# Seven block products in place of eight for eleven blocks of a feed-forward, with an encoder layer's residual put by in DRAM

## The chip, the cores and the metric

The kernel runs on one core of one Trainium2 chip. The metric is the device time of one execution in microseconds (us). TensorE (PE) multiplies into PSUM, VectorE (DVE) and ScalarE (ACT) do element-wise work, GpSimd (POOL) does some of it and issues the DMAs that add into SBUF, SyncE (SP) issues the plain DMAs.

## What is computed

One layer of a streaming encoder for 544 tokens (512 of a prompt and 32 of a sample) of width 1024. Three residual steps follow one another: a feed-forward, a mixer with two head groups, and a second feed-forward. The part that matters here is the last:

```python
def modulate(x, shift, scale):
    return x * (1.0 + scale[:, None, :]) + shift[:, None, :]

def post_norm(x, out, gate, weight, g, b):
    return layer_norm(ALPHA * x + weight * gate[:, None, :] * out, g, b)

def swiglu(h, w_gate, w_up, w_down):
    a = jnp.einsum('btd,df->btf', h, w_gate)
    u = jnp.einsum('btd,df->btf', h, w_up)
    return jnp.einsum('btf,fd->btd', jax.nn.silu(a) * u, w_down)
...
    x = post_norm(x, swiglu(modulate(x, sh3, sc3), f2_gate, f2_up, f2_down), 1.0 + gt3, 0.5, ln3_g, ln3_b)
```

The shifts, scales and gates come from a vector per request group times `w_cond`. `w_gate` and `w_up` are 1024 x 2816.

## The kernel before

Everything is float32. An operand of a product is split into two float32r parts, hi and lo, and a product is the sum of three matmuls, hi x hi, hi x lo and lo x hi (`mm3`, L139). The activations are kept turned, features on the partitions: `h` is eight tiles of 128 features by 2 parts by 544 tokens. A matmul has a 128x128 weight block as its stationary operand and 272 tokens (one half, `HALVES`) as the moving one, and PSUM gathers over the eight feature blocks.

The hidden width of 2816 is 22 blocks `f` of 128. For each block `ffn_up` (L193) makes four products of 24 matmuls, gate and up for both halves (`ffn_mm`, L172), and then `ffn_act` (L183) for each half: tanh of the gate on ACT (L187), two passes on DVE that make silu times up (L188, L189), a copy of its hi part on ACT (L190) and the lo part by subtraction on DVE (L191), into `hid[f]`. Blocks 0 and 1 of the second feed-forward are made together, half by half, by `k_outer` (L164), as `h` comes out of the layer norm. After block 21 the down products read all of `hid` (`proj_residual`, L205) and add into the residual `xr`.

Weights come through one queue, `stream`. `ensure` (L149) takes the next ones, loads them with SP into the pool `wr` (3 buffers), splits them with `split_w` (L123) into the pool `wh` (5 buffers), and `next_w` keeps three splits ahead. A split is a copy to hi on ACT (L129), minus hi into lo on ACT (L133), and a DMA issued by POOL that adds the raw weights from DRAM to lo (L134); with `lo_eng` a subtraction on that engine (L136) takes the place of the last two. Tiles of one size (4352 bytes per partition) share a pool `up` of 35 buffers: `h`, `hid`, `xr` and others. PSUM has eight banks, by tag: three a, two l, two t, one o.

The order of PE's instructions is that of the program (`ordered`, L66), and so is that of the loads on SP (`load`). On the other engines a planner orders the instructions by their place in the program and by when their inputs are due; `keep_in_program_order` pins an instruction behind the one written before it on its engine. Work beside the products is written as generators: `spawn` starts one, `tick` (L93), called after each product of 24 matmuls, moves on those that are due, and a `yield n` waits for n ticks.

Two such jobs run beside blocks 2 to 7 of the second feed-forward: `residual` (L1164), which scales the residual for the last layer norm with two POOL passes (L358) and two ACT passes (L360) per tile and four tiles, and `cond((8, (2, 3)))`, which loads eight tiles of `w_cond` and multiplies and adds them on DVE (L546) for the last gate.

Of the kernel before, what the change touches and what calls it, by code (L numbers as in the profile page):

```python
# [21 lines left out]
T = TP + TS  # L22
HT = T // 2
# [10 lines left out]
AHEAD = 3  # L34


@with_exitstack
def encoder_layer_kernel(ctx, tc, xT, cT, wc1, w_cond, b_condT, lnp, w_gu1, w_dn1, w_in, w_out, w_gu2, w_dn2,
                         ckT, cv, cikT, s0, cmat, ropes, dec, csm,
                         yT, akT, avT, ikT, st_p, st_s):  # L40
    nc = tc.nc
    ctx.enter_context(nc.allow_low_precision("operands are split exactly into two float32r parts"))
    const = ctx.enter_context(tc.tile_pool(name="const", bufs=1))
    up = ctx.enter_context(tc.tile_pool(name="up", bufs=35))
    wr = ctx.enter_context(tc.tile_pool(name="wr", bufs=3))
    wh = ctx.enter_context(tc.tile_pool(name="wh", bufs=5))
# [19 lines left out]
    def ordered(kind, r):  # L66
        if kind in last:
            tc.add_manual_dep(r.ins, last[kind], NOSYNC, reason="order of issue")
        last[kind] = r.ins.name

    def load(*a):
        ordered("load", nc.sync.dma_start(*a))

    def mm(*a, **kw):
        ordered("pe", nc.tensor.matmul(*a, **kw))  # L75
# [9 lines left out]
    def resume(job, base):  # L85
        n = next(job, None)
        if n is not None:
            jobs.append((base + n, job))

    def spawn(job):  # L90
        resume(job, now[0] + 1)

    def tick():  # L93
        now[0] += 1
        due = [j for t, j in jobs if t <= now[0]]
        jobs[:] = [x for x in jobs if x[0] > now[0]]
        for job in due:
            resume(job, now[0])
# [19 lines left out]
    def fetch_w(src, n, name):  # L118
        raw = wr.tile([P, ND, P], F32, name=f"wr_{name}", tag="wr")
        load(raw[:, :n, :], src)  # L120
        return raw

    def split_w(raw, n, name, lo_eng=None, pool=None, pin=False, src=None):  # L123
        if pool is None:
            hl = wh.tile([P, 2, ND, P], FR, name=f"wh_{name}", tag="wh")
            hi, lo = hl[:, 0], hl[:, 1]
        else:
            hi, lo = (pool.tile([P, ND, P], FR, name=f"wu_{name}", tag="u") for _ in range(2))
        c = nc.scalar.copy(hi[:, :n, :], raw[:, :n, :])  # L129
        if pin:  # L130
            tc.keep_in_program_order(c)
        if src is not None and lo_eng is None:
            nc.scalar.mul(lo[:, :n, :], hi[:, :n, :].bitcast(F32), -1.0)  # L133
            nc.gpsimd.dma_start(lo[:, :n, :], src, accum_op=ALU.add)  # L134
        else:
            (lo_eng or nc.gpsimd).tensor_tensor(lo[:, :n, :], raw[:, :n, :], hi[:, :n, :].bitcast(F32), op=ALU.subtract)  # L136
        return hi, lo
# [34 lines left out]
    def ffn_mm(st, h, which, i, tag=None):  # L172
        hls, banks = st
        if hls[which] is None:
            hls[which] = next_w()
        a, b = HALVES[i]
        ps = bank(tag or ("a" if which == 0 else "lt"[i]), f"gu{which}_{i}")[:, :HT]
        for k in range(ND):
            mm3(ps, hls[which], k, h[k], a, b, k == 0, k == ND - 1)
        banks[which, i] = ps  # L180
        tick()

    def ffn_act(st, hid, i):  # L183
# [3 lines left out]
        nc.scalar.activation(t, pg, AF.Tanh, scale=0.5)  # L187
        nc.vector.scalar_tensor_tensor(t, t, 1.0, pg, op0=ALU.add, op1=ALU.mult)  # L188
        nc.vector.tensor_tensor(t, t, pu, op=ALU.mult)  # L189
        nc.scalar.copy(hid[:, 0, a:b], t)  # L190
# [14 lines left out]
    def proj_residual(act, xr, coef, order, finish, need=(), ahead={}, final=None):  # L205
# [148 lines left out]
    def residual_next(xr, rs, al, j):  # L354

        for i, (a, b) in enumerate(HALVES):
            rb = rs[i].unsqueeze(1).to_broadcast([P, 2, HT])
            tc.keep_in_program_order(nc.gpsimd.tensor_tensor(xr[j][:, :, a:b], xr[j][:, :, a:b], rb, op=ALU.mult))  # L358
# [114 lines left out]
    for d in range(ND):  # L473
# [7 lines left out]
        if d in (0, 1, 3, 7):  # L481
            n = (0, 1, 3, 7).index(d)
# [51 lines left out]
    def cond(*parts):  # L534
        n = 0
        for m, pace in parts:
            acc = [up.tile([P, 1024], F32, name=f"ca{m}_{r}", tag="u") for r in range(2)]
            for d in range(ND):
                w = up.tile([P, 1024], F32, name=f"wc{m}_{d}", tag="u")
                load(w, w_cond[d * P:(d + 1) * P, 1024 * m:1024 * m + 1024])  # L540
                for r in range(2):
                    c = cz[:, d, r:r + 1]
                    if d == 0:
                        nc.vector.tensor_scalar(acc[r], w, c, None, op0=ALU.mult)
                    else:
                        nc.vector.scalar_tensor_tensor(acc[r], w, c, acc[r], op0=ALU.mult, op1=ALU.add)  # L546
# [7 lines left out]
    hid = []  # L554
# [27 lines left out]
    xd = nc.dram_tensor("x_spill", [4, P, 2 * T], F32, kind="Internal").ap()  # L582
# [567 lines left out]
    h, rs, fin = ln_to_h(xr, G3, B3, "h3_", 3, 4)  # L1150
# [172 lines left out]
```

## Time and profile before

| | |
|---|---|
| median of 3 runs | 1194.61 us (1192.08 to 1195.61) |
| the profiled execution's own time | 1194.37 us |
| its span, first to last instruction | 1192.2 us |
| mean granted TensorE clock | 0.989 |
| PE busy | 1162.6 us, 98% of the span, 9427 matmuls |
| DVE, ACT, POOL busy | 666.8, 586.8 and 206.5 us |
| products of blocks 0 and 1, second feed-forward | up to 802.66 us |
| blocks 2 to 21 | 802.66 to about 1043.5 us |
| its down products | from there to about 1177 us |

A row of a group of instructions gives the line, engine, operation, the tiles written and read, the shapes and the count, then busy time in us and the mean duration of one in ns, then how long the engine was idle just before them and what ended most of that. A row of the timeline gives start and duration in us, and in brackets the idle time before and its releaser.

### The profile page before, as it was taken

The numbers are of one execution on the slowest core, as the hardware profiler recorded it, in microseconds if no ns is written. First come the engines' busy times: TensorE is split into PE (matmuls) and PEld (weight loads), VectorE is DVE, ScalarE is ACT, GpSimd is POOL, SyncE is SP. The second block draws the span as 40 slices with busy tenths as digits, with TensorE's granted clock in tenths as the row PEclk, the third lists the DMA queues.
The fourth block names the chain that finished last, engine by engine and source line by source line (L and its number), as shares of the span: only waits on it lengthen the run. The fifth ranks groups of instructions, "written<-read, shape, count | busy, mean of one in ns | idle before, by whom it ended". The sixth has DMA issues, their size and how long they took to land.

```text
span 1192.2 us, 22987 instructions
## 1 busy us (share of the span) xinstructions
PE 1162.6 (98%) x9427; PEld 1129.9 (95%) x9427; DVE 666.8 (56%) x1567; ACT 586.8 (49%) x987; POOL 206.5 (17%) x234
## 2 busy tenths in 40 slices
PE   8999999999999999899989999999999999999995
PEld 6999999999999999789979989999999999999995
DVE  5756574763468394677887775896542222201416
ACT  3544444444334454655565678546444444433423
POOL 1311111111111303322110101105111111111110
PEclk9999999999999999899989999999999999999998
DMA  9899999987999557544845588817987888788842
GB/s 364 295 303 275 243 266 233 244 220 176 299 258 227 129 203 186 135 116 116 200 96 156 126 267 216 201 48 191 265 179 173 177 174 174 164 172 177 176 86 76
DMA packets 70953, 231.93 MB, mean 195 GB/s; under 512 B 8544, under 2 KB 12768, under 8 KB 70848
## 3 DMA queue, kind: packets, MB, share of 16 engines
q0 software_dynamic: 23616, 83.90, 40.4%
q1 hardware_dynamic: 47088, 146.43, 35.2%
q8 instruction: 74, 1.21, 0.4%
q14 instruction: 31, 0.25, 0.1%
q10 hardware_dynamic: 144, 0.14, 0.0%
HBM read 221.06 MB, written 7.35 MB: 192 GB/s over the span
## 4 chain that ended last, share of the span: by engine, by line
PE 90%; DVE 4%; DMA 3%; ACT 1%; issue 1%; SPq 0%; DVEq 0%; ACTq 0%
PE gu L75 41%; PE dn L75 26%; PE in L75 14%; PE gu_e L75 2%; DMA wc<-in_wc 1%; PE po L75 1%; PE pt L78 1%; DMA xr<-in_xT 1%; PE ro L75 1%; DMA rp<-iqf 1%; PE lg L75 1%; PE isc L75 1%; ACT wh_w L129 0%; DMA cm<-in_cmat 0%; DVE wk L790 0%
## 5 line engine op out<-in xcount | busy, mean ns | idle before, releaser
L75 PE MATMUL gu<-h,wh_w 128*128 128x272 f32 x3840 | 482.5, 288 | 0.0
L75 PEld LDWEIGHTS gu<-h,wh_w 128*128 128x128 f32 x3840 | 481.4, 188 | 0.0
L75 PE MATMUL dn<-hid,wh_w 128*128 128x272 f32 x2112 | 266.7, 288 | 0.0
L75 PEld LDWEIGHTS dn<-hid,wh_w 128*128 128x128 f32 x2112 | 265.4, 188 | 0.2
L129 ACT CAST wh_w<-wr_w 128x1024 fp32r<-128x1024 f32 (+1 forms) x162 | 165.8, 1024 | 148.0 <-PE dn L75 101.7
L75 PE MATMUL in<-h,wh_w 128*128 128x272 f32 x1392 | 190.7, 295 | 0.0
L75 PEld LDWEIGHTS in<-h,wh_w 128*128 128x128 f32 x1392 | 180.4, 192 | 5.3 <-issue 3.4
L133 ACT ACTIVATE wh_w<-wh_w 128x1024 fp32r<-128x1024 f32 x159 | 164.7, 1037 | 2.9
L546 DVE SCALAR_TENSOR_TENSOR ca<-wc,cz,ca 128x1024 f32<-128x1024 f32 x98 | 128.7, 1339 | 24.7 <-DMA wc<-in_w_cond 24.6
L134 POOL DMA_DIRECT2D wh_w<-in_w_gu x80 | 70.1, 876 | 415.8 <-ACT wh_w L133 356.6
L189 DVE TENSOR_TENSOR tnh<-tnh,gu 128x272 f32<-128x272 f32 x81 | 35.4, 437 | 129.5 <-PE gu L75 129.5
L187 ACT ACTIVATE tnh<-gu 128x272 f32<-128x272 f32 x80 | 31.9, 399 | 115.2 <-PE gu L75 115.2
L190 ACT CAST hid<-tnh 128x272 fp32r<-128x272 f32 x88 | 36.8, 419 | 93.9 <-DVE tnh L189 93.8
L188 DVE SCALAR_TENSOR_TENSOR tnh<-tnh,gu 128x272 f32<-128x272 f32 x80 | 34.7, 436 | 85.8 <-ACT tnh L187 85.6
L134 POOL DMA_DIRECT2D wh_w<-in_w_dn x48 | 41.7, 869 | 224.0 <-ACT wh_w L133 219.9
L269 DVE SCALAR_TENSOR_TENSOR xq<-dn,C,xq 128x272 f32<-128x272 f32 (+2 forms) x48 | 18.0, 403 | 105.0 <-PE dn L75 105.0
L191 DVE TENSOR_TENSOR hid<-tnh,hid 128x272 fp32r<-128x272 f32 x88 | 38.6, 440 | 37.2 <-ACT hid L190 36.8
L134 POOL DMA_DIRECT2D wh_w<-in_w_in x29 | 25.5, 893 | 135.2 <-ACT Pu L950 29.5
L789 DVE MAX8 m<-wk 128x8 f32<-128x544 f32 (+3 forms) x65 | 38.8, 597 | 0.7
L790 DVE MATCH_REPLACE8 wk<-m,wk 128x544 f32<-128x544 f32 (+3 forms) x65 | 38.0, 584 | 0.0
L75 PE MATMUL dn<-mx,wh_w 128*128 128x272 f32 x192 | 25.1, 289 | 0.0
L75 PE MATMUL in<-h,wu_w 128*128 128x272 f32 x192 | 24.6, 289 | 0.0
(274 smaller groups left out, 1118.4 us busy)
## 6 DMA issues: line engine op xcount, KB each, us to landing
wr_w<-in_w_gu SPq DMA_DIRECT2D x84, 512.0 KB, 5.2
wh_w<-in_w_gu POOLq DMA_DIRECT2D x80, 512.0 KB, 7.2
wc<-in_w_cond SPq DMA_DIRECT2D x56, 512.0 KB, 6.5
wr_w<-in_w_in SPq DMA_DIRECT2D x33, 512.0 KB, 5.2
wh_w<-in_w_in POOLq DMA_DIRECT2D x29, 512.0 KB, 6.8
wr_w<-in_w_dn SPq DMA_DIRECT2D x32, 448.0 KB, 4.1
wh_w<-in_w_dn POOLq DMA_DIRECT2D x32, 448.0 KB, 5.8
wc<-in_wc SPq DMA_DIRECT2D x16, 512.0 KB, 10.4
```

The costliest lines, as they stand in the source:

```text
L75: ordered("pe", nc.tensor.matmul(*a, **kw))
L129: c = nc.scalar.copy(hi[:, :n, :], raw[:, :n, :])
L133: nc.scalar.mul(lo[:, :n, :], hi[:, :n, :].bitcast(F32), -1.0)
L134: nc.gpsimd.dma_start(lo[:, :n, :], src, accum_op=ALU.add)
L187: nc.scalar.activation(t, pg, AF.Tanh, scale=0.5)
L188: nc.vector.scalar_tensor_tensor(t, t, 1.0, pg, op0=ALU.add, op1=ALU.mult)
L189: nc.vector.tensor_tensor(t, t, pu, op=ALU.mult)
L190: nc.scalar.copy(hid[:, 0, a:b], t)
L191: nc.vector.tensor_tensor(hid[:, 1, a:b], t, hid[:, 0, a:b].bitcast(F32), op=ALU.subtract)
L546: nc.vector.scalar_tensor_tensor(acc[r], w, c, acc[r], op0=ALU.mult, op1=ALU.add)
L789: behind(nc.vector.max(m8, w), "pe")
L790: nc.vector.match_replace(w, in_to_replace=m8, in_values=w, imm_value=MARK)
```

## The change

For blocks 4 to 14 (`SEVEN`) the gate and the up product of a block for both halves are taken together as a 2x2 by 2x2 block product: the weights are gate and up by lower and upper four feature blocks, the activations are lower and upper four feature blocks by first and second half. Eight block products of 12 matmuls become seven, by Winograd's scheme with sums of weights and sums of activations. `activation_sums` makes eight tiles of sums from `h` once. For each block `weight_sums` makes four sums on DVE in place, in the raw tiles, after `make_up` has copied and negated the upper half of up; `split_sums` splits the sums by a copy on ACT and a subtraction on DVE; `make_gate` splits the whole gate as before. Products share PSUM banks: the first product of a block stays in bank A, ACT takes a snapshot of it, and the next product adds into the same bank, three times over; B takes two products, C one. Every instruction of ACT and DVE in these blocks is pinned in the order written.

Besides, `xr` is written to DRAM six ticks after block 1 (`put_by`), and `bring_back` loads it again after block 19 and does the residual's scaling then; `cond` for the last gate starts after block 15 instead of block 2; and the low parts of the gates of blocks 15 to 21 and the up of block 15 are subtracted by DVE. The diff, cut where a reader can do without:

```diff
     def ensure(n):
-        while len(split) < n and stream:
+        while len(split) < n and stream and stream[0]:
+            if not fetched:
+                fetch_ahead()
             src, cnt, kw = stream.pop(0)
-            split.append(split_w(fetch_w(src, cnt, "w"), cnt, "w", src=src, **kw))
+            split.append(split_w(fetched.pop(0), cnt, "w", src=src, **kw))
...
+                queue_w(w_gu[f, which], lo_eng=nc.vector if which == 0 or f == skip[1] + 1 else None)
...
+    sums = [unit("hs", FR) for _ in range(ND)]
+    def activation_sums():
+        yield 0
+        for k in range(4):
+            ta, tb = sums[k], sums[4 + k]
+            la, lb = scr("la"), scr("lb")
+            for x, l in ((h[k], la), (h[4 + k], lb)):
+                nc.vector.tensor_tensor(l, x[:, 0].bitcast(F32), x[:, 1].bitcast(F32), op=ALU.add)
+            for o, p, q in ((la[:, 0:HT], la[:, HT:T], la[:, 0:HT]), (la[:, HT:T], lb[:, HT:T], la[:, HT:T]),
+                            (lb[:, HT:T], lb[:, HT:T], la[:, 0:HT]), (lb[:, 0:HT], lb[:, 0:HT], lb[:, HT:T])):
+                nc.vector.tensor_tensor(o, p, q, op=ALU.subtract)
+            for x, l in ((ta, la), (tb, lb)):
+                nc.scalar.copy(x[:, 0], l)
+                nc.vector.tensor_tensor(x[:, 1], l, x[:, 0].bitcast(F32), op=ALU.subtract)
+            yield 2
...
+    def negated(hi, raw, lo, src):
+        pin(nc.scalar.copy(hi, raw))
+        pin(nc.scalar.mul(lo, hi.bitcast(F32), -1.0))
+        nc.gpsimd.dma_start(lo, src, accum_op=ALU.add)
...
+    def weight_sums(f):
+        a11, a12, a21, a22 = (r[f][:, s] for r in (raw_g, raw_u) for s in (LO, HI))
+        for o, x, y, op in ((a22, a21, a22, ALU.add), (a21, a11, a21, ALU.subtract), (a11, a22, a11, ALU.subtract),
+                            (a12, a12, a11, ALU.subtract)):
+            pin(nc.vector.tensor_tensor(o, x, y, op=op))
+    def split_sums(f, W, raw):
+        W[f] = wh.tile([P, 2, ND, P], FR, name="wh_s", tag="wh")
+        pin(nc.scalar.copy(W[f][:, 0], raw[f]))
+        pin(nc.vector.tensor_tensor(W[f][:, 1], raw[f], W[f][:, 0].bitcast(F32), op=ALU.subtract))
+    def product(ps, W, w0, act, k0, i, start, stop):
+        a, b = HALVES[i]
+        for k in range(4):
+            for n, (x, y) in enumerate(((0, 0), (0, 1), (1, 0))):
+                mm(ps, W[:, x, w0 + k, :], act[k0 + k][:, y, a:b], start=start and not k and not n,
+                   stop=stop and k == 3 and n == 2, skip_group_check=True)
...
+    def begin(f):
+        A[f] = bank("a", "pA")[:, :HT]
+        product(A[f], Wg[f], 0, h, 0, 0, True, True)
+        s1[f] = snapshot(A[f], "s1")
+    def seven(f, hid):
+        t, u = scr("tnh", [P, 2, HT]), scr("up", [P, 2, HT])
+        if f + 3 <= last7:
+            load_gate(f + 3)
...
+        if f + 2 <= last7:
+            load_up(f + 2)
+        C = bank("l", "pC")[:, :HT]
+        product(C, Wg[f], 4, h, 4, 0, True, True)
+        pin(nc.vector.tensor_tensor(u[:, 0], s1.pop(f), C, op=ALU.add))
+        pin(nc.scalar.activation(t[:, 0], u[:, 0], AF.Tanh, scale=0.5))
+        tick()
+        product(A[f], Wg2[f], 0, sums, 4, 1, False, True)
+        s2 = snapshot(A[f], "s2")
+        pin(nc.vector.scalar_tensor_tensor(t[:, 0], t[:, 0], 1.0, u[:, 0], op0=ALU.add, op1=ALU.mult))
+        B = bank("t", "pB")[:, :HT]
+        product(B, Wu2[f], 0, sums, 0, 1, True, True)
+        if f < last7:
+            make_up(f + 1)
+            weight_sums(f + 1)
+        if f + 2 <= last7:
+            make_gate(f + 2)
+        else:
+            ensure(len(split) + 1)
+        tick()
+        product(A[f], Wu2[f], 4, sums, 0, 0, False, True)
+        s4 = snapshot(A[f], "s4")
+        pin(nc.vector.tensor_tensor(u[:, 1], s4, B, op=ALU.add))
+        if f < last7:
+            begin(f + 1)
+            split_sums(f + 1, Wg2, raw_g)
+        else:
+            ensure(len(split) + 1)
+            ffn_mm(plain, h, 0, 0)
+        tick()
+        product(A[f], Wg2[f], 4, h, 4, 1, False, True)
+        pin(nc.scalar.activation(t[:, 1], A[f], AF.Tanh, scale=0.5))
+        pin(nc.vector.scalar_tensor_tensor(t[:, 1], t[:, 1], 1.0, A.pop(f), op0=ALU.add, op1=ALU.mult))
+        if f < last7:
+            split_sums(f + 1, Wu2, raw_u)
+        product(B, Wu[f], 0, sums, 4, 0, False, True)
+        pin(nc.vector.tensor_tensor(u[:, 0], s2, B, op=ALU.add))
+        pin(nc.vector.tensor_tensor(t, t, u, op=ALU.mult))
+        t = t.rearrange("p a t -> p (a t)")
+        pin(nc.scalar.copy(hid[:, 0], t))
+        pin(nc.vector.tensor_tensor(hid[:, 1], t, hid[:, 0].bitcast(F32), op=ALU.subtract))
+        tick()
...
-    spawn(residual())
+    spawn(put_by())
...
-        if f == 2:
-            spawn(cond((8, (2, 3))))
...
+        if f == first7 - 1:
+            begin(first7)
+        if f == last7 + 1:
+            spawn(cond((8, (1, 2))))
+        if f == 19:
+            spawn(bring_back())
```

In the order of PE a block is: C; second product into A; first into B; third into A; the first product of the next block into its own A (`begin`); the last into this block's A; the second into B. `snapshot` is a pinned copy on ACT from PSUM to SBUF; the three of a block are s1, s2 and s4. The first sums, splits and gates (blocks 4 and 5) are made during block 3.

More of the change, by code (lines that the diff above doesn't have):

```diff
@@ L34 @@
 AHEAD = 3
+SEVEN = (4, 14)
 @with_exitstack
@@ L147, in encoder_layer_kernel, with fetch_ahead @@
     split = []
+    fetched = []
+    def fetch_ahead():
+        src, cnt, kw = stream[len(fetched)]
+        fetched.append(fetch_w(src, cnt, "w"))
     def ensure(n):
-        while len(split) < n and stream:
+        while len(split) < n and stream and stream[0]:
+            if not fetched:
+                fetch_ahead()
             src, cnt, kw = stream.pop(0)
-            split.append(split_w(fetch_w(src, cnt, "w"), cnt, "w", src=src, **kw))
+            split.append(split_w(fetched.pop(0), cnt, "w", src=src, **kw))
     def next_w(ahead=AHEAD):
@@ L395, in encoder_layer_kernel, with queue_ffn @@
     OUT = [(d, 0, 8, i) for i in range(2) for d in range(ND)]
-    def queue_ffn(w_gu, w_dn, f0, first=False):
+    def queue_ffn(w_gu, w_dn, f0, first=False, skip=None):
         for f in range(f0, NF):
+            if skip and f <= skip[1]:
+                if f < skip[0]:
+                    for which in range(2):
+                        queue_w(w_gu[f, which])
+                if f == skip[0]:
+                    stream.append(None)
+                continue
             for which in range(2):
+                if skip:
+                    queue_w(w_gu[f, which], lo_eng=nc.vector if which == 0 or f == skip[1] + 1 else None)
+                    continue
                 queue_w(w_gu[f, which], lo_eng=nc.gpsimd if first and f == f0 and which == 0 else None)
@@ L1155, in encoder_layer_kernel @@
     sts = [([next_w(0), next_w(0)], {}) for f in range(2)]
+    sums = [unit("hs", FR) for _ in range(ND)]
[13 more added lines that the diff above has]
+            yield 2
     for i in range(2):
+        if i:
+            spawn(activation_sums())
         for f in range(2):
@@ L1162, in encoder_layer_kernel, with put_by, bring_back @@
             ffn_act(sts[f], hid[f], i)
-    def residual():
-        yield 2
+    def put_by():
+        yield 6
         for j in range(4):
-            residual_next(xr, rs, al2, j)
-            yield 1
-    spawn(residual())
+            nc.sync.dma_start(xd[j], xr[j].rearrange("p a t -> p (a t)"))
+    def bring_back():
+        yield 0
+        xs = [unit(f"xs{j}") for j in range(4)]
+        for j in range(4):
+            load(xs[j].rearrange("p a t -> p (a t)"), xd[j])
+        yield 3
+        for j in range(4):
+            residual_next(xs, rs, al2, j)
+            yield 1
+        back.extend(xs)
@@ new lines, in encoder_layer_kernel, with load_gate, load_up @@
+    back = []
+    pin = tc.keep_in_program_order
+    LO, HI = slice(0, 4), slice(4, 8)
+    raw_g, raw_u, Wg, Wu, Wg2, Wu2 = {}, {}, {}, {}, {}, {}
+    def load_gate(f):
+        raw_g[f] = fetch_w(w_gu2[f, 0], ND, "g")
+    def load_up(f):
+        raw_u[f] = up.tile([P, ND, P], F32, name="wr_u", tag="u")
+        load(raw_u[f], w_gu2[f, 1])
+    def negated(hi, raw, lo, src):
+        pin(nc.scalar.copy(hi, raw))
+        pin(nc.scalar.mul(lo, hi.bitcast(F32), -1.0))
+        nc.gpsimd.dma_start(lo, src, accum_op=ALU.add)
@@ new lines, in make_gate, with make_up @@
+    def make_gate(f):
+        Wg[f] = wh.tile([P, 2, ND, P], FR, name="wh_g", tag="wh")
+        negated(Wg[f][:, 0], raw_g[f], Wg[f][:, 1], w_gu2[f, 0])
+    def make_up(f):
+        Wu[f] = up.tile([P, 2, 4, P], FR, name="wh_u", tag="u")
+        negated(Wu[f][:, 0], raw_u[f][:, HI], Wu[f][:, 1], w_gu2[f, 1][:, HI])
+    def weight_sums(f):
[3 more added lines that the diff above has]
+            pin(nc.vector.tensor_tensor(o, x, y, op=op))
@@ new lines, in snapshot @@
+    def snapshot(ps, name):
+        s = half_scr(name)
+        pin(nc.scalar.copy(s, ps))
+        return s
+    first7, last7 = SEVEN
+    A, s1 = {}, {}
+    def begin(f):
[7 more added lines that the diff above has]
+        else:
+            fetch_ahead()
+        if f + 2 <= last7:
[24 more added lines that the diff above has]
+            split_sums(f + 1, Wg2, raw_g)
+        else:
+            ensure(len(split) + 1)
[13 more added lines that the diff above has]
+        tick()
@@ L1171, in encoder_layer_kernel, with pass_bar @@
+    plain = [None, None], {}
+    def pass_bar():
+        assert stream.pop(0) is None
+    spawn(put_by())
     for f in range(2, NF):
         hid.append(unit("hid", FR))
-        ffn_up(h, hid[f])
-        if f == 2:
-            spawn(cond((8, (2, 3))))
+        if f == first7 - 2:
+            load_gate(first7)
+            load_up(first7)
+        if f == first7 - 1:
+            load_gate(first7 + 1)
+            load_up(first7 + 1)
+            load_gate(first7 + 2)
+        if first7 <= f <= last7:
+            if f == first7:
+                pass_bar()
+            seven(f, hid[f])
+            continue
+        st = plain if f == last7 + 1 else ([None, None], {})
+        for which in range(2):
+            for i in range(2):
+                if (which, i) not in st[1]:
+                    ffn_mm(st, h, which, i)
+                if f == first7 - 1:
+                    if which == 0 and i == 0:
+                        make_gate(first7)
+                        make_up(first7)
+                    if which == 0 and i == 1:
+                        weight_sums(first7)
+                    if which == 1 and i == 0:
+                        split_sums(first7, Wg2, raw_g)
+                        split_sums(first7, Wu2, raw_u)
+                        make_gate(first7 + 1)
+        for i in range(2):
+            ffn_act(st, hid[f], i)
+        if f == first7 - 1:
+            begin(first7)
[3 more added lines that the diff above has]
+            spawn(bring_back())
@@ L1176, in encoder_layer_kernel @@
+    xr = back
+    assert len(xr) == 4
     known(8)
```

2 lines of the change are left out of this document (1 added, 1 removed).

## The prediction

> **What bounds the kernel now.** I read the page first (busy shares, the chain that ended last), then the busy time by stretches, then the groups of instructions between 826.8 and 959.4 us, and last the timeline around single hand-overs.
>
> ```profile
> PE 1162.6 (98%) x9427; PEld 1129.9 (95%) x9427; DVE 666.8 (56%) x1567; ACT 586.8 (49%) x987; POOL 206.5 (17%) x234
> PE 90%; DVE 4%; DMA 3%; ACT 1%; issue 1%; SPq 0%; DVEq 0%; ACTq 0%
> 790.00:802.66 12.66, 12.37 (x98) 12.00 (x97) 10.37 (x37) 6.55 (x21) 0.00 (x0) 1.00 0.00 1
> 802.66:814.70 12.04, 12.04 (x99) 12.04 (x98) 3.46 (x9) 6.78 (x12) 6.19 (x5) 1.00 0.53 132
> 814.70:826.80 12.10, 12.10 (x99) 12.10 (x98) 10.75 (x8) 8.59 (x12) 6.96 (x6) 1.00 0.57 145
> 826.80:959.40 132.60, 132.60 (x1061) 132.60 (x1060) 49.94 (x96) 63.20 (x92) 20.08 (x24) 1.00 0.86 203
> L75 PE MATMUL gu<-h,wh_w 128*128 128x272 f32 x1059 | 133.0, 288 | 0.0
> L75 PE MATMUL gu<-h,wh_w x1070: 282/288/371, 825.8 to 959.9; 128*128 128x272 f32 x179
> L133 ACT ACTIVATE wh_w<-wh_w 128x1024 fp32r<-128x1024 f32 x23 | 24.3, 1057 | 0.4
> L129 ACT CAST wh_w<-wr_w 128x1024 fp32r<-128x1024 f32 x22 | 23.0, 1043 | 16.8 <-PE gu L75 16.8
> L189 DVE TENSOR_TENSOR tnh<-tnh,gu 128x272 f32<-128x272 f32 x23 | 10.0, 437 | 37.3 <-PE gu L75 37.3
> L190 ACT CAST hid<-tnh 128x272 fp32r<-128x272 f32 x23 | 9.6, 419 | 17.3 <-DVE tnh L189 17.3
> L187 ACT ACTIVATE tnh<-gu 128x272 f32<-128x272 f32 x22 | 8.8, 399 | 32.9 <-PE gu L75 32.9
> ```
>
> A row of a stretch gives its length, then the busy time of PE, PEld, DVE, ACT and POOL, the granted clock, the DMA share and GB/s. Blocks 4 to 14 are the stretch 826.8 to 959.4: 11 blocks of 96 matmuls, 12.06 us each, PE never idle at clock 1.00, with DVE at 38% and ACT at 48%. A matmul lasts 288 ns (the row with three values gives least, median and most) but they overlap: 133.0 / 1059 = 0.1256 us each is the price of one. So this stage is PE's, and every matmul taken away pays until another engine becomes late.
>
> **The change, part by part.**
>
> *Matmuls.* A block goes from 96 to 7 x 12 = 84. That is 12 x 0.1256 = 1.51 us, x 11 = **16.6 us**, and PE's own block would be 10.55 us, each product 1.51 us.
>
> *What ACT and DVE get per block.* The rows for the shapes:
>
> ```profile
> L599 ACT COPY aqk<-in 128x272 f32<-128x272 f32 x16 | 6.1, 383 | 16.8 <-PE in L75 16.4
> L632 ACT CAST iqs<-iqf 128x512 fp32r<-128x512 f32 x4 | 2.4, 624 | 0.0
> L136 DVE TENSOR_TENSOR wh_w<-wr_w,wh_w 128x1024 fp32r<-128x1024 f32 x2 | 2.4, 1221 | 0.0
> L633 DVE TENSOR_TENSOR aqs<-aqk,aqs 128x512 fp32r<-128x512 f32 x4 | 2.7, 685 | 0.2 <-ACT aqs L632 0.2
> L305 DVE TENSOR_TENSOR xq<-xq,lnm 128x544 f32<-128x544 f32 x9 | 6.5, 721 | 0.0
> ```
>
> ACT before: 4 weight passes of 1.05 and 4 small ones, 5.8 us. After: three PSUM copies (0.38), two tanh (0.40), a 128x544 hid copy (0.42 for 272 and 1.04 for 1024 give 0.65), gate copy and negation (1.04, 1.06), half of up copied and negated (0.62 each), two copies of sums (1.04): about 8.1 us. DVE before: 6 x 0.44 = 2.6. After: five at 0.44, four weight sums at 0.69, two subtractions at 1.22, two 128x544 passes at 0.72: 8.8 us. Both still fit into 10.55. But they work in order, and their hand-overs form a ring, so totals don't decide.
>
> *The ring.* Its prices are start-to-start spacings:
>
> ```profile
> 709.93 1.22 DVE L136 TENSOR_TENSOR wh_w<-wr_w,wh_w 128x1024 fp32r<-128x1024 f32 x1
> 711.06 0.43 DVE L1141 SCALAR_TENSOR_TENSOR rgt<-rgt,in 128x272 f32<-128x272 f32 x1
> 717.23 3.24 PE L75 MATMUL in<-h,wh_w 128*128 128x272 f32 x24
> 720.50 0.40 ACT L1140 ACTIVATE rgt<-in 128x272 f32<-128x272 f32 x1 [1.18 <-PE in L75]
> 720.79 0.74 ACT L1126 ACTIVATE xq<-xq,ab 128x544 f32<-128x544 f32 x1
> 720.93 0.44 DVE L1141 SCALAR_TENSOR_TENSOR rgt<-rgt,in 128x272 f32<-128x272 f32 x1 [1.02 <-ACT rgt L1140]
> 721.40 0.44 DVE L1142 TENSOR_TENSOR rgt<-rgt,ret 128x272 f32<-128x272 f32 x1
> 721.88 0.42 ACT L996 CAST mx<-rgt 128x272 fp32r<-128x272 f32 x1
> 746.69 2.63 DVE L226 TENSOR_TENSOR xq<-xq,shc 128x544 f32<-128x544 f32 x4
> 819.33 1.04 ACT L129 CAST wh_w<-wr_w 128x1024 fp32r<-128x1024 f32 x1
> 820.40 1.06 ACT L133 ACTIVATE wh_w<-wh_w 128x1024 fp32r<-128x1024 f32 x1
> 821.37 0.38 ACT L187 ACTIVATE tnh<-gu 128x272 f32<-128x272 f32 x1
> ```
>
> A hand-over costs 0.03 to 0.04 us (PE's modelled end 720.47 to 720.50; 720.90 to 720.93; 721.84 to 721.88). A dependent pass on one engine starts 0.03 after the end (720.93 + 0.44 to 721.40; 819.33 + 1.04 to 820.40). An independent one starts 0.09 to 0.11 before it (709.93 to 711.06 is 1.13; 820.40 to 821.37 is 0.97; 720.50 to 720.79 is 0.29; four 128x544 passes in 2.63 are 0.64 apart). From the copy s4 of one block to that of the next, in the order that the pins write out:
> - s4 copies out of A 0.38, PE may add the sixth product 0.05, whose twelfth matmul ends 11 x 0.1256 + 0.288 = 1.67 later, hand-over 0.03: 2.13
> - second tanh 0.29, then copy of the Wu2 sums 1.08: 1.37
> - their subtraction on DVE 1.13; s2 + B 0.47; product of both halves 0.76: 2.36
> - hid copy on ACT 0.69, its subtraction on DVE 0.64: 1.33
> - s1 + C 0.48, first tanh 0.29, s2 copy 0.29: 1.06
> - up half copied 0.65 and negated 0.52; gate copied 1.07 and negated 0.97; then s4 again: 3.21
>
> Together **11.46 us**, more than PE's 10.55. PE has slack of one product between most copies and the next addition; at 11.46 it is used up, and PE waits before the fourth product (for s2, behind the tanh, behind s1 + C, behind the late hid subtraction) and the sixth (for s4, queued behind the gate's negation). The first block starts with slack and the last has no weights to make, so I count 9 blocks at 0.91 and one at half: 8.6 us lost. PE starting again after a wait has no clean row; a matmul of this stage took 371 ns at worst against 288, so I add 0.08 to each of 9 rings, 0.7 (bounds 0 and 2).
>
> *Sums of activations.* Four groups on DVE, each four 128x544 at 0.64 and four 128x272 at 0.36 (0.44 less the same 0.08): 4.0, together 16.0 us, and eight ACT copies. They stand ahead of the activations of blocks 0, 1 (second half) and 2. DVE has idle time from about 800.2 on (10.37 of 12.66 busy before 802.66, 3.46 of the next 12.04). Block 3 wants PSUM of block 2's first gate half at 814.7 + 3.0 = 817.7; by then DVE owes 16.0 + 2.8 us from 800.2, which is 819.0. I take 1.3 us of PE stall, bounds 0 (a planner that lets the activations go first) and 2.5 (all waits between them exposed).
>
> *Residual.* It goes to DRAM (4 stores of 544 KB on SP in block 3) and comes back in block 20 (4 loads on SP, in order with the weights, which are about two blocks ahead); its 8 POOL passes and 8 ACT passes move from blocks 2 and 3 to 20 and 21, where POOL's weight issues queue behind them and DVE can be held up. Cover: this is just what blocks 2 and 3 bear now.
>
> ```profile
> 818.87 8.31 DVE L546 SCALAR_TENSOR_TENSOR ca<-wc,cz,ca 128x1024 f32<-128x1024 f32 x2
> 820.45 5.64 POOL L358 TENSOR_TENSOR xq<-xq,lny 128x544 f32<-128x544 f32 x4
> 842.87 2.48 DVE L546 SCALAR_TENSOR_TENSOR ca<-wc,cz,ca 128x1024 f32<-128x1024 f32 x2
> 843.83 0.87 POOL L134 DMA_DIRECT2D wh_w<-in_w_gu  x1 [7.08 <-ACT wh_w L133]
> DMA to landing us min/median/max: 5.3/5.7/10.9
> ```
>
> Two DVE passes that take 2.48 us elsewhere took 8.31 beside POOL's passes, and PE was busy 12.10 of 12.10. So 0; without that cover some 6 us once. The Trainium skill ("SBUF — State Buffer", SBUF: two separate sides) says that a DVE pass with two SBUF inputs and a GpSimd pass that reads SBUF exclude each other for the whole instruction; by that rule, too, the seven-product blocks are free of it, since POOL only issues DMAs there. The trace agrees (7.1 us longest for one such pass; 2.48 for two beside an issue).
>
> *Conditioning (cond) to block 15, and DVE instead of ACT and POOL for the low parts of eight later weights.* DVE gains 1.22 each in blocks of 12.06 where it is 38% busy with cond: 0.
>
> *Weights.* Loads are a block and a half ahead. A gate's low part is negated at about 7.0 in a block, issued 0.4 later, and wanted by the fifth product of the next, at 16.6 or later; landing takes 5.7 us (10.9 with cond's loads beside it, which are gone here). 0; it binds only from a landing of about 9.2 us.
>
> **Sum.** -16.6 + 8.6 + 0.7 + 1.3 = -6.0 us. The profiled execution took 1194.4 (span 1192.2 and 2.2 around it), 0.2 below the median of 1194.6; the forecast is **1188.4 us**.
>
> **Rivals.**
> *PE stays the bound.* If the ring closes in 10.55 or less, all 16.6 come through: 1194.4 - 16.6 + 1.3 = 1179. It needs 8% off every step; the spacings were read to about 0.02 us, but the 128x512 and 128x544 steps are interpolated. Chance 0.15.
>
> *Slower: dear hand-overs.* The ring changes engine six times at 0.03 to 0.05. If one change costs 0.20, for an instruction that waits for two engines or a PE that restarts cold, the ring is 12.5 and the eleven blocks take 10.55 + 9 x 12.5 + 11.5 = 134.6; with 1.3 at the entry that is 3.3 more than now, about 1198. That is where slower by over 0.3% begins; at 0.3 it is 1203. The rows show no such price, but no row shows these instructions. Chance 0.15.
>
> *No change to be measured.* A ring of 11.9, or an entry stall of 4: the gain falls to some 3 us, about 1191.5. 0.3% (3.6 us) is about what a measurement here tells from nothing. Chance 0.18.
>
> *The clock drops at the short stops.*
>
> ```profile
> 470.00:500.00 30.00, 27.07 (x196) 24.20 (x194) 20.50 (x44) 17.49 (x32) 15.06 (x16) 0.89 0.65 175
> 600.00:610.00 10.00, 6.50 (x28) 5.38 (x27) 8.21 (x22) 4.23 (x11) 1.57 (x5) 0.66 0.62 140
> 690.00:710.00 20.00, 18.01 (x161) 15.41 (x161) 14.99 (x63) 15.43 (x36) 1.74 (x2) 1.00 0.88 272
> ```
>
> PE idle 35% of a stretch ran at 0.66; at 10% idle one stretch has 0.89 and one, with shorter stops, 1.00. I expect 8% in stops of half a microsecond. At 0.89 PE's block would be 11.9 and the time about 1193, so it is inside the third case, at 0.02. The Trainium skill ("TensorE: Matmul & The Clock Gate", A second HAM failure mode: psum-queue depth-cycling) says that PE idling briefly between groups of products can make the clock swing between half and full; by that rule the forecast falls to this case, and the trace bears it out in two of the three stretches.
>
> **Chances and range.** My ring (1183 to 1190.8) has 0.50 and PE-bound 0.15, so faster 0.65 (the rest of the ring's spread is in the third case); same 0.18 with the clock inside; slower 0.17, the rival and 0.02 for late weights. Range 1179 to 1198: it reaches the PE-bound case below and the start of the slower one above, leaving about 0.2.
>
> **What would show it.** Right: 84 matmuls per block, about 11.4 to 11.6 us per block, two PE stops in each, before the product that follows s2 and before that after s4, both released by ACT, and DVE and ACT each near 75% there. Matmuls at 0.1256 and no stops: the first rival. Blocks over 12.1 with stops at hand-overs: the second. A stop near 818: the sums. PE waiting for wh_g's DMA or anything in blocks 20 and 21 would be a step that I priced at nothing.

## The result, and the profile after

The changed kernel takes 1211.9 us (median of 4 runs, 1208.2 to 1212.8) against 1194.9 for the kernel before (4 runs, 1192.1 to 1195.6): 1.0145 times as long, 95% interval 1.013 to 1.0159. The forecast was 1188.4 with a range up to 1198. The profiled execution took 1212.8, with a span of 1210.5; the span before was 1192.2. So there are 18.3 us to find between the spans, and 24.4 between the forecast and the profiled execution.

First the page of the changed kernel: busy time, the chain that ended last, and the group of matmuls that waited longest.

```profile
PE 1154.3 (95%) x9295; PEld 1117.4 (92%) x9295; DVE 758.2 (63%) x1684; ACT 604.3 (50%) x1031; POOL 199.4 (16%) x226
PE 77%; issue 8%; DVE 6%; ACT 5%; DMA 3%; SPq 0%; POOL 0%; DVEq 0%; POOLq 0%; ACTq 0%
L76 PE MATMUL gu<-h,wh_w 128*128 128x272 f32 x2784 | 353.5, 290 | 19.7 <-ACT wh_w L130 11.8
```

132 matmuls are gone, as planned (9427 to 9295), but PE's share of the chain fell from 90% to 77%. The group that lost the time is not one of the new products: `gu` with `wh_w` are the plain blocks, and 19.7 us of idle PE stand before them. The busy time by stretches of the changed kernel (length; PE, PEld, DVE, ACT, POOL; clock; DMA share; GB/s) shows where:

```profile
790.00:803.00 13.00, 12.71 (x99) 12.21 (x98) 13.00 (x42) 6.87 (x22) 0.00 (x0) 1.00 0.46 162
803.00:815.00 12.00, 0.23 (x3) 0.08 (x1) 11.89 (x26) 5.17 (x10) 0.00 (x0) 0.59 0.00 0
815.00:827.00 12.00, 4.05 (x16) 3.73 (x17) 4.08 (x8) 8.50 (x10) 2.79 (x4) 0.50 0.90 223
827.00:840.00 13.00, 13.00 (x99) 13.00 (x98) 2.64 (x6) 2.59 (x5) 0.70 (x1) 0.92 0.61 159
...
873.56:954.54 80.98, 77.27 (x591) 74.20 (x589) 60.14 (x91) 51.38 (x86) 12.17 (x14) 1.00 0.67 161
```

The same place before, 802.66 to 826.80, is quoted in the prediction: PE without a gap at clock 1.00. PE's timeline in the changed kernel names the two stops there, and beside them the stops inside a steady block and the two longest later ones:

```profile
814.92 0.82 PE L76 MATMUL gu<-h,wh_w 128*128 128x272 f32 x2 [11.77 <-ACT wh_w L130]
823.69 26.43 PE L76 MATMUL gu<-h,wh_w 128*128 128x272 f32 x190 [7.95 <-DMA wh_w<-in_w_gu]
...
890.09 1.76 PE L76 MATMUL pA<-hs,wh_s 128*128 128x272 f32 x12 [0.31 <-ACT s L1262]
893.57 1.77 PE L76 MATMUL pA<-h,wh_s 128*128 128x272 f32 x12 [0.23 <-ACT s L1262]
901.65 1.76 PE L76 MATMUL pA<-hs,wh_s 128*128 128x272 f32 x12 [0.30 <-ACT s L1262]
...
960.52 1.78 PE L76 MATMUL pA<-hs,wh_s 128*128 128x272 f32 x12 [1.31 <-ACT s L1262]
972.96 1.76 PE L76 MATMUL pA<-hs,wh_s 128*128 128x272 f32 x12 [1.65 <-ACT s L1262]
```

PE waits for the first weight of block 2: 11.77 us for its hi part and, after two matmuls, 7.95 for its lo part. The 192 matmuls of blocks 2 and 3 then take 0.82 + 26.43 = 27.25 us in place of 24.1, because the granted clock has fallen to 0.50 and is back at 1.00 only at about 829, some 5 us after PE goes on. The Trainium skill ("TensorE: Matmul & The Clock Gate", HAM oscillation — how this bites in real kernels) says that a PE idle for more than some 3.4 us drops to half clock; this stop, with 0.50 behind it, agrees. Blocks 2 and 3 end at 849.95 and not at 826.8, 23.1 us late.

The rest is the gain. From there to the end of block 14 at 980.55, less the 24 matmuls of block 15 that are made there (3.0 us), the eleven blocks take 127.6 us in place of 132.6. 23.1 - 5.0 = 18.1, which leaves 0.2 of the difference of the spans.

**Why the weight was late.** SP's own timeline, first before and then after (the stretch 727 to 760 before holds nine loads of one group). `wr_w` is a raw weight of the plain blocks, `wr_g` and `wr_u` are the raw gate and up of a seven-product block, and `x_spill<-xq` are the stores of `put_by`:

```profile
727.29 33.27 SPq L72 DMA_DIRECT2D wr_w<-in_w_gu  x9
```

```profile
727.49 7.77 SPq L73 DMA_DIRECT2D wr_w<-in_w_gu  x4
736.58 0.33 SPq L73 DMA_DIRECT2D wr_g<-in_w_gu  x1
784.94 3.32 SPq L1204 DMA_DIRECT2D x_spill<-xq  x4
788.37 1.00 SPq L73 DMA_DIRECT2D wr_u<-in_w_gu  x1
789.42 27.82 SPq L73 DMA_DIRECT2D wr_w<-in_w_gu  x4
```

and from the waits of the changed kernel (us in total, times, longest):

```profile
SPq L1204 <- DVE lnz L324: 48.4, 1, 48.4
```

In the changed program `load_gate(4)` and `load_up(4)` are written at the top of block 2, ahead of the `ensure` that fetches the weights of blocks 2 and 3, and loads keep the program's order. `put_by`'s stores, written six ticks after block 1, are in no such order and stand ahead of `wr_u`; they wait 48.4 us for the layer norm's last writes. So the load of block 2's first weight, which was the fifth of the nine before and was issued at 736.2, is issued at 789.42. It lands some 7 us later, still ahead of 803. But ACT (`la` and `lb` are activation sums, `hs` their split parts):

```profile
803.17 0.64 ACT L1187 CAST hs<-la 128x544 fp32r<-128x544 f32 x1
804.95 0.65 ACT L1187 CAST hs<-lb 128x544 fp32r<-128x544 f32 x1 [1.14 <-DVE lb L1185]
806.74 0.64 ACT L1187 CAST hs<-la 128x544 fp32r<-128x544 f32 x1 [1.14 <-DVE la L1185]
...
808.53 0.65 ACT L1187 CAST hs<-lb 128x544 fp32r<-128x544 f32 x1 [0.82 <-DVE lb L1185]
...
813.28 0.64 ACT L1187 CAST hs<-la 128x544 fp32r<-128x544 f32 x1 [2.54 <-DVE la L1185]
813.83 1.04 ACT L130 CAST wh_w<-wr_w 128x1024 fp32r<-128x1024 f32 x1
```

The split (L130) stands in ACT's order behind five copies of activation sums, four of which wait (1.14, 1.14, 0.82 and 2.54 us) for a DVE that is busy 11.89 of 12.00 us. In the kernel before, the same split is this row of ACT's timeline:

```profile
755.24 1.05 ACT L129 CAST wh_w<-wr_w 128x1024 fp32r<-128x1024 f32 x1 [1.75 <-PE dn L75]
```

That gave the theory: a late load led to a late place on ACT, behind the sums. Its rivals: the sums cost by themselves; the late load costs by itself; the moved residual or the new blocks cost.

### The profile page after: what moved, and what is told of

It reads as the page before. It is cut to its first block, busy times and chain, and to the rows that moved or that the text cites. A ratio compares the mean times of both kernels' runs of the same rounds, so it can differ in the third digit from the quotient of the medians.

```text
span 1210.5 us, 22941 instructions
## 1 busy us (share of the span) xinstructions
PE 1154.3 (95%) x9295; PEld 1117.4 (92%) x9295; DVE 758.2 (63%) x1684; ACT 604.3 (50%) x1031; POOL 199.4 (16%) x226
## 4 chain that ended last, share of the span: by engine, by line
PE 77%; issue 8%; DVE 6%; ACT 5%; DMA 3%; SPq 0%; POOL 0%; DVEq 0%; POOLq 0%; ACTq 0%
PE gu L76 29%; PE dn L76 23%; PE in L76 15%; PE pA L76 1%; PE gu_e L76 1%; DMA wc<-in_wc 1%; DVE wh_s L1251 1%; PE po L76 1%; PE pt L79 1%; DMA xr<-in_xT 1%; ACT wh_s L1250 1%; PE ro L76 1%; ACT wh_g L1231 1%; ACT wh_g L1230 1%; PE lg L76 1%
## 5 line engine op out<-in xcount | busy, mean ns | idle before, releaser
L76 PE MATMUL gu<-h,wh_w 128*128 128x272 f32 x2784 | 353.5, 290 | 19.7 <-ACT wh_w L130 11.8
L76 PEld LDWEIGHTS gu<-h,wh_w 128*128 128x128 f32 x2784 | 351.8, 190 | 20.2 <-ACT wh_w L130 12.0
L130 ACT CAST wh_w<-wr_w 128x1024 fp32r<-128x1024 f32 (+1 forms) x140 | 142.9, 1021 | 117.3 <-PE dn L76 100.0
L134 ACT ACTIVATE wh_w<-wh_w 128x1024 fp32r<-128x1024 f32 x129 | 133.0, 1032 | 2.4
L135 POOL DMA_DIRECT2D wh_w<-in_w_gu x50 | 43.6, 873 | 334.2 <-ACT wh_w L134 262.3
L197 DVE TENSOR_TENSOR tnh<-tnh,gu 128x272 f32<-128x272 f32 x59 | 25.8, 437 | 82.6 <-PE gu L76 82.6
L198 ACT CAST hid<-tnh 128x272 fp32r<-128x272 f32 x66 | 27.6, 418 | 95.5 <-DVE tnh L197 95.4
L196 DVE SCALAR_TENSOR_TENSOR tnh<-tnh,gu 128x272 f32<-128x272 f32 x58 | 24.9, 435 | 36.3 <-ACT tnh L195 36.2
L76 PE MATMUL pA<-hs,wh_s 128*128 128x272 f32 x264 | 37.5, 291 | 5.4 <-ACT s L1262 5.4
L76 PEld LDWEIGHTS pA<-hs,wh_s 128*128 128x128 f32 x264 | 34.1, 188 | 7.6 <-ACT s L1262 7.6
```

## The experiments

Each run stands beside the kernel before, whose median in these runs was 1193.8 (first four) and 1193.7 us (last four).

### The entry

**e1_loads_first** puts the fetches of blocks 2 and 3 back ahead:

```diff
         if f == first7 - 2:
+            ensure(4)
             load_gate(first7)
             load_up(first7)
```

> The four weights of blocks 2 and 3 are queued ahead of the gate and up of block 4; the four residual stores then stand behind them on SP. My theory: the 20.5 us stop of PE at 803 to 824 comes from block 2's weights, which in the changed kernel are loaded 30 us later than before, and is split in two links (SP order, then ACT order behind the activation sums). With the loads first, both links go: the splits of blocks 2 and 3 run at 755 to 768 as before, PE stops at most 1.3 us near 818 for the sums, and the eleven blocks stay as in the changed kernel (11.57 us each): 1211.9 - 20.5 - 2.5 (slow clock behind the long stop) + 0 to 1.3 = 1189 to 1190.5 us. Rival A, the sums themselves are what costs (16 us on a DVE that is 100% busy from 790 to 815): a stop of 8 us or more stays, 1198 or above. Rival B, the seven-product blocks or the moved residual lose it: no change, 1209 or above.

Measured: 1191.8 us, ratio 0.998 (0.9968 to 0.9992). One line is worth 20 us. The split is back at its place on ACT and PE runs through 803 to 825.87; the sums' 16 us on DVE stop it nowhere. The first stop is now a later one:

```profile
753.85 1.05 ACT L130 CAST wh_w<-wr_w 128x1024 fp32r<-128x1024 f32 x1 [1.75 <-PE dn L76]
827.61 1.53 PE L76 MATMUL pA<-h,wh_g 128*128 128x272 f32 x10 [1.74 <-DMA wh_g<-in_w_gu]
```

Rivals A and B fall. The load had been 53 us late in the changed kernel (736.2 to 789.4) and not 30, as I had put it. The time is 1 to 3 us above what I expected, for this stop at `begin(4)` and another of 0.35 at the next, for the low parts of the first two gates, which had been hidden behind the long stop.

**e2_stores_behind** moves only the stores, behind the loads:

```diff
     def put_by():
         yield 6
         for j in range(4):
-            nc.sync.dma_start(xd[j], xr[j].rearrange("p a t -> p (a t)"))
+            load(xd[j], xr[j].rearrange("p a t -> p (a t)"))
```

> Only the four residual stores move: they are issued in the order of the loads, behind those of blocks 2 and 3; gate and up of block 4 still stand ahead of block 2's weights. The up weight of block 4 waits for a buffer of the common pool, which I think the out-projection's operands free at about 777 when their last product ends. Theory: block 2's first load is then issued at about 778 and not at 789, but its split on ACT is still planned behind the copies of the sums, so nearly nothing is won: 1207 to 1212 us. Rival, the stores are the whole cause (every microsecond that the load comes earlier is a microsecond of PE's stop): 11 us less, about 1199 to 1201.

Measured: 1212.3 us, ratio 1.0142 (1.012 to 1.0164), 0.3 above the theory's range and far from the rival's. From its timelines of SP, ACT and PE:

```profile
774.26 0.86 SPq L73 DMA_DIRECT2D wr_w<-in_w_gu  x2
812.65 0.65 ACT L1187 CAST hs<-la 128x544 fp32r<-128x544 f32 x1 [2.54 <-DVE la L1185]
813.21 1.04 ACT L130 CAST wh_w<-wr_w 128x1024 fp32r<-128x1024 f32 x1
823.22 26.07 PE L76 MATMUL gu<-h,wh_w 128*128 128x272 f32 x190 [8.10 <-DMA wh_w<-in_w_gu]
```

The load is issued 15 us earlier and the split is not: it waits in line on ACT from the landing, at 774.26 + 4.8 (the median of the two loads), to 813.21. The up weight's buffer, free at 773.84, holds the load back nearly as well as the stores did.

**e3_stores_ahead** does the opposite: the stores go into the loads' order ahead of all of block 2's loads, `load_gate(4)` and `load_up(4)` behind them.

```diff
     def put_by():
-        yield 6
+        yield 0
         for j in range(4):
-            nc.sync.dma_start(xd[j], xr[j].rearrange("p a t -> p (a t)"))
+            load(xd[j], xr[j].rearrange("p a t -> p (a t)"))
...
-    spawn(put_by())
+    for _ in put_by():
+        pass
...
         if f == first7 - 2:
+            ensure(4)
             load_gate(first7)
```

> The four residual stores stand ahead of all weights of block 2 on SP, on purpose, and gate and up of block 4 behind those of blocks 2 and 3. Block 2's loads are thus as late as in the changed kernel (issued at about 788), but the planner now puts block 2's split on ACT ahead of the copies of the sums. Theory (the late load alone is a small part, ACT's order behind the sums is the large one): raw weight at about 795, split by 798, its low part added by about 805, so PE stops 1.5 to 4 us at 803 and the time is 1191 to 1195 us. Rival (the late load on SP is the whole cause): the stop stays near 20 us, 1207 or above.

```profile
788.40 8.44 SPq L73 DMA_DIRECT2D wr_w<-in_w_gu  x4
795.46 1.03 ACT L130 CAST wh_w<-wr_w 128x1024 fp32r<-128x1024 f32 x1
806.95 25.59 PE L76 MATMUL gu<-h,wh_w 128*128 128x272 f32 x190 [3.44 <-DMA wh_w<-in_w_gu]
```

Measured: 1196.3 us, ratio 1.0027 (1.0011 to 1.0042). The load is as late as in the changed kernel, but the split runs at 795.46 and PE's stop is 3.44 us. The stop is inside the theory's bounds, the time 1.3 above them: the clock between 803 and 815 is 0.86, and the gates of blocks 4 and 5 are waited for (1.49 and 0.52 us) as in e1.

**e4_sums_late** leaves SP as it is and starts the sums later:

```diff
     for i in range(2):
-        if i:
-            spawn(activation_sums())
...
     spawn(put_by())
+    spawn(activation_sums())
```

> SP's order is left as in the changed kernel; the job that makes the activation sums is started after the products of blocks 0 and 1, so only one copy of sums stands ahead of block 2's split on ACT where five did. Theory (ACT's order behind the sums is the larger link): the split runs at 800 to 804, its low part is added by 807 to 812, PE stops 4 to 10 us, 1195 to 1203 us. Rival (the late load alone): no change, 1207 or above.

```profile
788.79 18.46 SPq L73 DMA_DIRECT2D wr_w<-in_w_gu  x4
802.25 0.40 ACT L195 ACTIVATE tnh<-gu_e 128x272 f32<-128x272 f32 x1 [0.35 <-PE gu_e L76]
802.75 0.65 ACT L1187 CAST hs<-la 128x544 fp32r<-128x544 f32 x1
803.63 1.04 ACT L130 CAST wh_w<-wr_w 128x1024 fp32r<-128x1024 f32 x1
813.42 25.83 PE L76 MATMUL gu<-h,wh_w 128*128 128x272 f32 x190 [8.18 <-DMA wh_w<-in_w_gu]
```

Measured: 1202.0 us, ratio 1.0057 (1.0038 to 1.0075), inside the theory's range; the stops are 2.20 + 8.18 = 10.4 us, 0.4 above theirs. One copy of sums is left ahead of the split. The last tanh passes of blocks 0 and 1, which wait for PE, stand there too.

Side by side, in us:

| | load issued | split on ACT | PE goes on | PE's stop | time |
|---|---|---|---|---|---|
| before | 736.2 | 755.2 | | 0 | 1194 |
| changed | 789.4 | 813.8 | 823.7 | 19.7 | 1211.9 |
| e2 | 774.3 | 813.2 | 823.2 | 19.9 | 1212.3 |
| e4 | 788.8 | 803.6 | 813.4 | 10.4 | 1202.0 |
| e3 | 788.4 | 795.5 | 807.0 | 3.4 | 1196.3 |
| e1 | 734.8 | 753.9 | | 0 | 1191.8 |

PE goes on 9.8 to 11.5 us after the split begins (its two passes, POOL's issue, the landing of 7 us), whatever the load did. The stop follows the split's place on ACT. The late load alone costs e3's 3.4 us; the remaining 16 of 19.7 are ACT's order. They have two parts. Starting the sums later, with one copy ahead of the split and not five, is worth 19.7 - 10.4 = 9.3 us (e4 against the changed kernel). The other 10.4 - 3.4 = 7.0 go with the place behind the last activations of blocks 0 and 1, which the split still has in e4 and no longer in e3.

A load as late as the changed kernel's went with an early split in e3, and one 15 us earlier with a late split in e2. So the time of the load doesn't by itself set the split's place, as the theory had it.

The Trainium skill ("PSUM — Partial Sum Buffer", Engine vs sequencer instructions) calls the queues of ScalarE, VectorE and GpSimd strictly first in, first out. e2's rows agree: ACT idles 2.54 us before the copy at 812.65, while the weight that its next pass splits has lain there since 779.

### The ring

**e5_neg_late** takes one pass out of the ring, with the loads as in e1: `gate_hi` makes the gate's copy alone in the old place, and `gate_lo`, the negation and its DMA, comes after s4.

```diff
-            make_gate(f + 2)
+            gate_hi(f + 2)
...
         s4 = snapshot(A[f], "s4")
+        if f + 2 <= last7:
+            gate_lo(f + 2)
```

> Loads of blocks 2 and 3 first, as in e1_loads_first, and one pass of the ring moved: the negation of the gate two blocks ahead is pinned on ACT behind the copy s4 and no longer ahead of it. Theory (the ring of hand-overs sets the block): PE stops no longer before the sixth product; what is left is the loop through s2, by the spacings of the prediction 3.02 + 1.70 + 1.37 + 2.36 + 1.33 + 1.20 = 10.98 us, and with the 0.12 that the trace showed over the working 11.1 us per block, one stop of about 0.5 us in each, before the fourth product. Against 1191.8 us some 0.47 x 10 less: 1186.5 to 1188. Rival (the stops come from PE or PSUM, for instance from a first matmul that starts late after any change of bank): 11.57 us per block stays, 1191 to 1192.5.

**e6_neg_tanh** also copies s2 ahead of the first tanh:

```diff
-        pin(nc.scalar.activation(t[:, 0], u[:, 0], AF.Tanh, scale=0.5))
         tick()
         product(A[f], Wg2[f], 0, sums, 4, 1, False, True)
         s2 = snapshot(A[f], "s2")
+        pin(nc.scalar.activation(t[:, 0], u[:, 0], AF.Tanh, scale=0.5))
```

> As e5_neg_late, and the copy s2 is pinned on ACT ahead of the first tanh of its block and no longer behind it, so that the fourth product doesn't wait for the subtraction of the block before. Theory: no loop of hand-overs longer than PE's own 10.55 us is left (10.3 by the spacings); blocks of 10.55 to 10.7 us without regular stops, 10 x 0.9 to 1.0 less than e1_loads_first: 1181 to 1183 us. Rival (another queue becomes the bound at once, DVE's with 8.8 us per block or the landing of the gate's low part): blocks of 11 us or more, 1186 or above.

Measured: e5 1189.1 us, ratio 0.9964 (0.9951 to 0.9977); e6 1183.6, ratio 0.992 (0.9905 to 0.9935). Both times are above what I expected, by 1.1 and 0.6 us. Two of e5's stops, then the busy time of six steady blocks each, first of e5, then of e6:

```profile
879.90 1.77 PE L76 MATMUL pA<-hs,wh_s 128*128 128x272 f32 x12 [0.32 <-ACT s L1270]
890.98 1.77 PE L76 MATMUL pA<-hs,wh_s 128*128 128x272 f32 x12 [0.31 <-ACT s L1270]
```

```profile
863.85:930.30 66.45, 64.57 (x506) 63.27 (x505) 50.59 (x79) 44.04 (x74) 10.43 (x12) 1.00 0.72 167
```

```profile
863.23:927.16 63.93, 63.93 (x506) 63.46 (x505) 50.36 (x79) 42.73 (x73) 10.43 (x12) 1.00 0.72 173
```

66.45 / 6 = 11.08 us per block with one stop, before the fourth product; the loop through s2 gave 11.1. 63.93 / 6 = 10.66 without a stop, where PE's own time was put at 10.55. So the two loops are what made the block 11.57, and PE or PSUM are not. A stop costs more than its row says: 11.08 - 10.66 = 0.42 us per block for one of 0.31, at a granted clock of 1.00. The excess over the expected times is again outside the steady blocks: e5 and e6 wait 2.7 and 2.5 us for the first two gates, and 1.32 + 1.69 and 0.22 + 1.04 us near the end.

### The moves alone, and all together

**e8_moves_alone** keeps the residual's and the conditioning's new places and takes the seven products out, with all that belongs to them:

```diff
-    queue_ffn(w_gu2, w_dn2, 2, skip=SEVEN)
+    queue_ffn(w_gu2, w_dn2, 2)
...
-        if first7 <= f <= last7:
...
-            seven(f, hid[f])
-            continue
```

> The rest of the change alone: residual put by in DRAM and brought back after block 19, conditioning after block 15, all blocks with eight products, no sums, low parts added by DMA as before. Theory (these moves cost nothing where the loads of blocks 2 and 3 keep their place): within 0.3% of the kernel before, 1191 to 1197 us, PE busy without a stop over 1 us from 803 us to the down products. Rival (the residual's passes and reloads in blocks 20 and 21, or the stores, cost some microseconds): 1198 or above.

Measured: 1194.9 us, ratio 1.0021 (1.0003 to 1.0038): a cost of 0.4 to 4.5 us by the interval, inside the theory's range, that no stretch of the trace shows. PE is whole where the residual and cond were and where they went:

```profile
803.00:815.00 12.00, 12.00 (x98) 12.00 (x97) 2.64 (x6) 5.54 (x8) 1.76 (x2) 1.00 0.84 175
852.00:940.00 88.00, 88.00 (x705) 88.00 (x704) 18.89 (x43) 41.19 (x59) 12.21 (x14) 1.00 0.83 174
965.00:1032.00 67.00, 67.00 (x537) 67.00 (x536) 38.93 (x57) 32.99 (x48) 15.51 (x16) 1.00 0.86 233
```

**e9_all** adds to e6 the two ends of the stretch: the splits of block 4's gate and up two products earlier, in block 2, their sums one product earlier, and the splits for block 15 at the end of blocks 13 and 14.

```diff
+                if f == first7 - 2 and which == 1 and i == 0:
+                    make_gate(first7)
+                    make_up(first7)
                 if f == first7 - 1:
                     if which == 0 and i == 0:
-                        make_gate(first7)
-                        make_up(first7)
+                        weight_sums(first7)
...
-        else:
-            ensure(len(split) + 1)
         tick()
         product(A[f], Wu2[f], 4, sums, 0, 0, False, True)
...
         pin(nc.vector.tensor_tensor(hid[:, 1], t, hid[:, 0].bitcast(F32), op=ALU.subtract))
+        if f + 2 > last7:
+            ensure(len(split) + 1)
```

> As e6_neg_tanh, and the two places where e1_loads_first still showed PE waiting: the gate and up of block 4 are split in block 2 and their sums begun a product earlier (there were stops of 1.74 and 0.35 us for the low part of a gate at 826 and 836), and in blocks 13 and 14 the splits for block 15 stand at the end of the block (stops of 1.32 and 1.68 us before a fourth product, with the subtraction of such a split on DVE ahead of it). Theory: another 2 to 4 us less than e6_neg_tanh, 1177.5 to 1180.5 us, near the 1179 that PE's matmuls alone would give. Rival (the late stops are already gone with s2 ahead of the tanh, and the early gate only collides with the activation sums on DVE): no better than e6_neg_tanh.

Measured: 1180.9 us, ratio 0.9894 (0.988 to 0.9909), the best of all and faster than both kernels. Its stops of PE in blocks 2 to 21 are these two:

```profile
831.53 1.77 PE L76 MATMUL pA<-hs,wh_s 128*128 128x272 f32 x12 [1.10 <-ACT s L1270]
837.11 1.52 PE L76 MATMUL pA<-h,wh_g 128*128 128x272 f32 x10 [0.55 <-DMA wh_g<-in_w_gu]
```

It is 2.7 us below e6, and 0.4 above the range that I gave. 1179, the rival in which PE's matmuls decide, is 1.9 us away; these two stops are 1.65.

## Why the prediction was wrong

*Matmuls, right.* 84 per block; at 63.93 / 506 = 0.1263 us each where nothing stops PE (0.1256 predicted).

*The ring, right in mechanism and size.* 11.54 us predicted, 11.57 measured, with the two stops at the two products named, and DVE and ACT at 74% and 63% (60.14 and 51.38 of 80.98; "near 75%" was too high for ACT). The hand-overs are as cheap as the rows said, and the rival of dear ones has no support. The last 0.08 of the 11.54 was taken from one long matmul, so a miss of only 0.03 is partly luck. The prediction wrote out one loop; with its negation moved, e5 shows a second one, through s2, of 11.08 us, which was hidden under the first. e6 moves one more pass and shows 10.66 without a stop.

*The clock at the short stops, right.* Two stops of 0.2 to 0.3 us in each block left it at 1.00. So the rule of the Trainium skill ("TensorE: Matmul & The Clock Gate", A second HAM failure mode: psum-queue depth-cycling) on a PE that idles briefly between groups of products did not apply here.

*The sums, wrong in kind.* 1.3 us of stop at PSUM near 818 was predicted. e1 shows none: DVE makes up its arrears in time. What they cost in the changed kernel is something else, the place of five of their copies ahead of the split: 9.3 us of stop between this kernel and e4.

*The step that failed.* "Loads are a block and a half ahead" stood for the steady blocks and was taken for the entry too; "So 0" for the residual looked at POOL, DVE and the reloads, and put the stores in block 3, since they are written six ticks after block 1. The trace has them at 784.94, ahead of block 2, and SP stood waiting at them for the 48.4 us before. I never wrote out SP's order around block 2, although `load_gate` and `load_up` are new instructions on a queue that keeps its order, and never asked what ACT's copies of sums would stand in front of. In place of the 0 there is a PE that stops 19.7 us and then runs 3.1 us longer at the lowered clock. This one omission is 23.1 - 1.3 = 21.8 of the 24.4 us. "Slower by late weights" had a chance of 0.02.

*The last blocks, undersized.* Blocks 13 and 14 were counted at losses of 0.99 and 0.46 us against PE's own time. They lost 1.56 and 1.86, with the two long stops: subtractions for block 15 stand there on DVE ahead of the ring's passes (L137, one in block 13 and two in block 14; the prediction had these subtractions at 0). That is 2.0 us; with 0.2 for the ring it makes up the difference between a gain of 7.3 and one of 5.0. e1 has the same stop of 1.68 us in block 14 and these rows on DVE ahead of it; e9, where the splits stand at the end of the blocks, has no stop there:

```profile
946.42 1.22 DVE L137 TENSOR_TENSOR wh_w<-wr_w,wh_w 128x1024 fp32r<-128x1024 f32 x1
948.19 1.22 DVE L137 TENSOR_TENSOR wh_w<-wr_w,wh_w 128x1024 fp32r<-128x1024 f32 x1
```

With the entry mended the sum would have been nearly right and the forecast still not: e1 gains 2.0 us by the medians (3.4 by the spans) and not 6.0, by the last blocks' 2.0 and by 2.1 for the first two gates, less the 1.3 of the sums. The gates are the same step once more: "0" for a gate's low part was worked out for a steady block, and the gate of block 4 is negated only in block 3, some 5 us before PE wants it.

What stays open: why the planner gives the split its place behind the sums was not tried by itself. In e1 and e3, where the fetches come first in the program, the split stands ahead of them; in e2, where only the stores move, it does not.

## What to carry to other kernels

When a change adds loads or stores, write out the order of the queue that issues them around the first place where the stage begins, and for each one what it waits for and what stands behind it; a store that waits for data holds up loads that wait for nothing. When it adds work on an engine that also prepares weights, ask where the preparation now stands in that engine's order: the same sums cost 0 behind the splits (e1) and, ahead of one, 9.3 us of a stopped PE that starting them later gave back (e4). A ring of hand-overs can be worked out from start-to-start spacings to 0.1 us per block, and then it also tells which single pass to move: two moved passes brought the block from 11.57 to 10.66.

## What the runs showed of the hardware

A stop of 11.77 us, two matmuls and another of 7.95 cost 3.1 us beyond themselves, since the granted clock was 0.50 to 0.59 there and 0.92 in the 13 us after. A single stop of 1.74 us (e1) or 1.99 (e5) left the clock at 1.00 from 820 to 860; after the one of 3.44 us in e3 it was 0.86 from 803 to 815.

Two stops of 0.2 to 0.3 us in every 11.57 left the clock at 1.00 but cost more than their rows say: 11.57 - 10.66 = 0.91 us per block for 0.53 of idle time. A group of twelve matmuls is shown as 1.66 us long where the next one starts 1.50 after it, so part of the wait is hidden in the row before; and the group behind a stop takes 1.76 to 1.78.

In e2, 34 us lay between the landing of a raw weight and its first pass on ACT, which was busy 14.86 us of them, and PE stopped 19.9 us: a weight that has landed is not yet one that PE can use.
